# Three norm passages of a two-layer decoder: late squares go to the sums unadded, and some steps of one half get an order against the other half's

## The chip, the cores and the metric

The kernel runs on one core of a Trainium2 chip. The metric is the time of one execution on the device, in microseconds (us). TensorE is called PE below, its weight loads PEld, VectorE DVE, ScalarE ACT, GpSimd POOL, and SyncE, which issues the loads from memory, SP.

## The reference

A trunk of two layers over 512 tokens of width 1024, in float32. Each layer has a token mixer (layer 0: a diagonal state space and a gated linear recurrence side by side; layer 1: gated linear attention, GLA) and a SwiGLU feed-forward part. Each of these sub-layers starts with the same norm, and ends in a gated addition to the trunk `x`:

```python
def rms_norm(x, g):
    xf = x.astype(jnp.float32)
    y = xf * lax.rsqrt(jnp.mean(xf * xf, axis=-1, keepdims=True) + EPS)
    return (y * g.astype(jnp.float32)).astype(x.dtype)

def modulate(h, shift, scale):
    return h * (1 + scale[:, None, :]) + shift[:, None, :]
...
def swiglu(h, w1, w3, w2):
    return (jax.nn.silu(h @ w1) * (h @ w3)) @ w2
```

So between two sub-layers the sum of 1024 squares of each token has to be complete before the first product of the next sub-layer can be formed. `shift`, `scale` and the gate come from a conditioning vector.

## The kernel before

The trunk is held transposed: eight tiles `x0` to `x7` of 128 features by 512 tokens. Products are emulated float32: each weight and each activation is split into a high and a low part (`hi`, `lo`; `whi`, `wlo`; `hhi`, `hlo`), and three matmuls are made of them, hi by hi (line 275), hi by the activation's low part (276) and low weight by high activation (277). In the stretches of this case a matmul has 256 tokens, half of the sequence; `TH` are the two halves, z = 0 and z = 1, called the first and the second half.

Three norm passages are built by `norm_mod` and `norm_stats`, one for each half: f0, from the output projection of layer 0's mixer to its feed-forward part; m1, from that part to GLA; f1, from GLA's output projection to the second feed-forward part. The last two digits of a name give passage and half, so `nst_f01` is f0's second half. The steps of one half:

1. The projection's products end (`or`, or `f` in m1), DVE adds them to the trunk (`residual`, rows `x<-or,mod,x`), and ACT squares each of the eight tiles, `m` = 0 to 7 (line 86, `nsq`; the first two into the two halves of `na`).
2. Squares 2 to 6 are added into the two sums of `na` on POOL or DVE (line 107, `ttv`); square 7 is left as it is.
3. Three statistic parts (the two sums and square 7) go through PE against a matrix of ones and zeros `eb` (line 341, `nst<-eb,na` and `nst<-eb,nsq`). Each part is two matmuls, which run in two passes each, so the trace shows four records for a part.
4. ACT takes the root (`nrs`, line 86), DVE the reciprocal and one Newton step (`nnv`, reciprocal, `nnt`, `nnt`, `nrs`), and DVE writes the result on diagonals (`ndg`, line 111). A matmul against ones spreads them over the partitions (line 347, `nst<-ndg,ones`); it is called the spread below.
5. For each of the eight tiles DVE forms `hf`, ACT `hhi`, DVE `hlo` (lines 116, 86, 116), and the next products take them. In f0 and f1 the first of these are `f1` and `f3` (the two SwiGLU inputs, `whi_f`), in m1 `ga`, `gq` and `gk`.

The order of each engine's instructions isn't written out: a scheduler places them by priorities, by the order in the program and by its own timeline, and each engine then works its list in that order. `tc.issue_after` (used through `after`) and a manual dependency hold one instruction behind another on the list. ACT's function tables are loaded by `tact`, which keeps the table loads (line 101) and the functions that need them in a chain, `table["last"]`; the root of the norm is one such function, the next one is the SiLU of the feed-forward part or of GLA's gate. The squares and the sums of a half come from a pool of four buffers (tags "n" and "X"), the statistics of a half from PSUM.

In `out_rest` (f0 and f1) the whole weight is there when the halves begin; the first half's four pairs of tiles are projected, then `then` builds the first half's norm, then the second half follows.

Of the kernel before, what the change touches and what calls it, by code (L numbers as in the profile page):

```python
# [41 lines left out]
def trunk(  # L42
# [10 lines left out]
    out = out[0]  # L53
# [11 lines left out]
    def tt(name, tag, shape=(P, T), dtype=F32):  # L65
        return tp.tile(list(shape), dtype, tag=tag, name=name, bufs=SLOTS[tag])
# [4 lines left out]
    def const(name, shape, dtype=F32):  # L71
        return cp.tile(list(shape), dtype, name=name, tag=name)

    def mm_ps(name, shape=(P, T)):
        return pm.tile(list(shape), F32, tag="mm", name=name)

    def ps_a(name, shape=(P, T)):
        return pa.tile(list(shape), F32, tag="a", name=name)
# [4 lines left out]
    V, A, G, PE = nc.vector, nc.scalar, nc.gpsimd, nc.tensor  # L83

    def act(o, i, f, **kw):
        return A.activation(out=o, in_=i, func=f, **kw)  # L86

    table = {"set": None, "last": None}
    order = mybir.DependencyInfo(mybir.DependencyClass.NoSync, mybir.DependencyReason.DATA)
# [16 lines left out]
    def ttv(e, o, a, b, op):  # L106
        e.tensor_tensor(out=o, in0=a, in1=b, op=op)  # L107

    def tsv(e, o, a, s1, op0, s2=None, op1=None):
        if s2 is None:  # L110
            e.tensor_scalar(out=o, in0=a, scalar1=s1, scalar2=None, op0=op0)
        else:
            e.tensor_scalar(out=o, in0=a, scalar1=s1, scalar2=s2, op0=op0, op1=op1)

    def stt(o, a, s, b, op0, op1):
        V.scalar_tensor_tensor(out=o, in0=a, scalar=s, in1=b, op0=op0, op1=op1)  # L116


    cs = const("cs", [P, P + 2])
# [1 line left out]
    ident = cs[:, 0:P]  # L121
# [25 lines left out]
    ones = const("ones", [P, P])  # L147
    G.memset(ones, 1.0)
    eb = const("eb", [P, NB, NB])
# [17 lines left out]
    gsc = const("gsc", [P, 4, KT])  # L167
# [65 lines left out]
    def ada_need(*ps):  # L233
        while not done.issuperset(ps):
            next(ada)
# [3 lines left out]
    xT = [xp.tile([P, T], F32, name=f"x{m}", tag=f"x{m}") for m in range(KT)]  # L239
# [18 lines left out]
    def split(e, src, name, th, tl):  # L258
        hi = tt(f"hi_{name}", th, dtype=F32R)
        lo = tt(f"lo_{name}", tl, dtype=F32R)  # L260
        act(hi, src, AF.Copy)
        ttv(e, lo, src, hi.bitcast(F32), ALU.subtract)
        return hi, lo
# [5 lines left out]
    def proj(ps, ws, acts, ts=slice(0, T), ks=None):  # L269

        n = len(ws)
        for i, ((hi, lo), (ah, al)) in enumerate(zip(ws, acts, strict=True)):
            if ks and i not in ks:
                continue
            PE.matmul(ps, lhsT=hi, rhs=ah[:, ts], start=(i == 0), stop=False)  # L275
            PE.matmul(ps, lhsT=hi, rhs=al[:, ts], start=False, stop=False)  # L276
            ins = PE.matmul(ps, lhsT=lo, rhs=ah[:, ts], start=False, stop=(i == n - 1))  # L277
        return ins
# [29 lines left out]
    def inv_rms(name, ss, n, table=True):  # L308

        rs, t, v = (sm(f"{name}{i}", ss.shape) for i in ("rs", "nt", "nv"))  # L310
        if table:
            tact(rs, ss, AF.Sqrt, scale=1.0 / n, bias=eps)
        tsv(V, v, ss, 1.0 / n, ALU.mult, EPS, ALU.add)
        if table:
            V.reciprocal(out=rs, in_=rs)
        else:

            tsv(V, t.bitcast(I32), v.bitcast(I32), 1, ALU.logical_shift_right)
            tsv(V, rs.bitcast(I32), t.bitcast(I32), -1.0, ALU.mult, float(0x5F3759DF), ALU.add)
        for _ in range(1 if table else 3):  # L320
            ttv(V, t, rs, rs, ALU.mult)
            stt(t, t, -0.5, v, ALU.mult, ALU.mult)
            stt(rs, t, 1.5, rs, ALU.add, ALU.mult)
        return rs

    def norm_stats(name, z):

        ts, nb, pst, tag = TH[z], NB // 2, (ps_a, ps_b)[z], "nX"[z]
        sums = tt(f"na_{name}", tag, (P, 2, T // 2))
        for m in range(KT):  # L330
            sq = sums[:, m] if m < 2 else tt(f"nsq_{name}{m}", tag, (P, T // 2))
            act(sq, xT[m][:, ts], AF.Square)
            if 1 < m < KT - 1:
                i = int(m not in (2, 4))
                ttv(V if i and not z else G, sums[:, i], sums[:, i], sq, ALU.add)
        parts = [sums[:, 0], sums[:, 1], sq]
        ps = pst(f"nst_{name}", (P, nb + 1, P))
        rb, st = ps[:, 0:nb, :], ps[:, nb, 0:nb]
        for i, q in enumerate(parts):
            for b in range(nb):  # L340
                PE.matmul(st, lhsT=q[:, b * P : (b + 1) * P], rhs=eb[:, b, 0:nb],
                          start=(i == 0 and b == 0), stop=(i == len(parts) - 1 and b == nb - 1))
        rs = inv_rms("n", st, D)
        dg = tt(f"ndg_{name}", tag, (P, nb, P))
        for b in range(nb):
            tsv(V, dg[:, b, :], ident, rs[:, b : b + 1], ALU.mult)
            PE.matmul(rb[:, b, :], lhsT=ones, rhs=dg[:, b, :], start=True, stop=True)
        return rb.rearrange("p b t -> p (b t)")

    def norm_parts(name):  # L350
        hh = hp.tile([P, KT, T], F32R, tag="h", name=f"hhi_{name}", bufs=2)
        hl = hp.tile([P, KT, T], F32R, tag="h", name=f"hlo_{name}", bufs=2)
        return [(hh[:, m, :], hl[:, m, :]) for m in range(KT)]
# [9 lines left out]

    def norm_mod(q, l, base, name, parts, z):

        ada_need((l, base // 8), (l, base // 8 + 1))
        rb = norm_stats(f"{name}{z}", z)
        ts = TH[z]
        for m in range(KT):
            hh, hl = (i[:, ts] for i in parts[m])  # L370
            shift = mod[:, l, base + m : base + m + 1]
            hf = tt(f"hf_{name}{z}{m}", "nX"[z], (P, T // 2))
            stt(hf, rb, gsc[:, q, m : m + 1], xT[m][:, ts], ALU.mult, ALU.mult)
            act(hh, hf, AF.Identity, bias=shift)
            stt(hl, hf, shift, hh.bitcast(F32), ALU.add, ALU.subtract)

    def ada_first_loads(half):
        tags = iter("s" * 15 + "n")
        ws = []
        for k in range(KT):  # L380
            for i in (1, 0):
                w = tt(f"ar0{i}{half}{k}", next(tags))
                nc.sync.dma_start(out=w, in_=ada_w[0, k * P : (k + 1) * P, i * D + half * T : i * D + half * T + T])
                ws.append(w)
        return ws

    def after(ins):
        return tc.issue_after(ins.ins) if ins is not None else nullcontext()
# [504 lines left out]
    def out_rest(w, ys, l, then):  # L893

        n = len(ys)
        ws = []
        for k in range(n):
            raw = wp.tile([P, D], F32, tag="raw", name=f"raw_or{l}{k}", bufs=3)
            nc.sync.dma_start(out=raw, in_=w[D - (n - k) * P : D - (n - k - 1) * P, :])
            ws.append([split(V, raw[:, i * T : (i + 1) * T], f"or{l}{k}{i}", "s", "s") for i in range(D // T)])  # L900
        for z, ts in enumerate(TH):
            for m in range(0, KT, 2):
                ps = mm_ps(f"or{l}{m}{z}", (P, 2, T // 2))
                for j in (m, m + 1):
                    c = slice(j * P % T, j * P % T + P)
                    proj(ps[:, j - m], [tuple(q[:, c] for q in ws[k][j * P // T]) for k in range(n)], ys, ts)
                for j in (m, m + 1):
                    residual(ps[:, j - m], j, l, 2, ts)
            then(KT - 1, z)

    def then_norm(q, l, base, name, res):

        res += norm_parts(name)

        def then(m, z):
            if m == KT - 1 and z is not None:
                norm_mod(q, l, base, name, res, z)

        return then

# [24 lines left out]
    for m in range(KT):  # L945
        ps = mm_ps(f"xps{m}")
# [10 lines left out]
    for m in range(KT):  # L957
        ps = (mm_ps if m < 4 else ps_b)(f"xnps{m}")
# [9 lines left out]
    second = range(4, KT)  # L968
# [127 lines left out]
    ys = s5_glu(yfs)  # L1096
# [29 lines left out]
    ps = ps_a("ga1")  # L1126
# [20 lines left out]
    for hd in range(4):  # L1147
        ps = mm_ps(f"ga2{hd}")
# [12 lines left out]
        for i, z in enumerate((Q, K)):  # L1161
            ps, w = qk[i] if hd == 0 else gla_qk(hd, i)
# [98 lines left out]
```

## Time and profile before

| | us |
|---|---|
| Three timed runs | 1345.32, 1347.97, 1352.27 |
| Their median | 1347.97 |
| Profiled execution, own time | 1345.65 |
| Its span, first to last instruction | 1343.9 |
| PE busy in the span | 1280.0 |

All times of rows are microseconds from the start of the span of the profiled execution. In a row of the timeline the first number is the start, the second how long the group lasted, `x4` the number of records put together, and the bracket the idle time of that engine ahead of the row with what ended it. Matmuls overlap in their pipeline: a lone matmul of 256 columns shows 0.28 long, while the next one starts 0.12 after it, so what a step takes of PE is read from start to start.

### The profile page before, as it was taken

The numbers are of one execution on the slowest core, as the hardware profiler recorded it, in microseconds if no ns is written. First come the engines' busy times: TensorE is split into PE (matmuls) and PEld (weight loads), VectorE is DVE, ScalarE is ACT, GpSimd is POOL, SyncE is SP. The second block draws the span as 40 slices with busy tenths as digits, with TensorE's granted clock in tenths as the row PEclk, the third lists the DMA queues.
The fourth block names the chain that finished last, engine by engine and source line by source line (L and its number), as shares of the span: only waits on it lengthen the run. The fifth ranks groups of instructions, "written<-read, shape, count | busy, mean of one in ns | idle before, by whom it ended". The sixth has DMA issues, their size and how long they took to land.

```text
span 1343.9 us, 18265 instructions
## 1 busy us (share of the span) xinstructions
PE 1280.0 (95%) x6949; PEld 1097.6 (82%) x6949; DVE 766.8 (57%) x1433; ACT 514.1 (38%) x939; POOL 141.4 (11%) x148
## 2 busy tenths in 40 slices
PE   7797999899999999999999999999899999999997
PEld 3577887778888888888888999997888888888886
DVE  5786995787765566566356446657743333333344
ACT  5477358534522222232244433433432222222322
POOL 0593451110100000000010000000100000000000
PEclk9798998999999999999999999999799999999999
DMA  9742531633097669996250322114033323333232
GB/s 305 173 126 79 157 110 38 152 98 102 20 223 189 186 183 230 205 219 185 74 157 21 102 65 78 56 48 133 17 98 103 97 71 99 113 99 104 65 92 79
DMA packets 222824, 159.69 MB, mean 119 GB/s; under 512 B 16752, under 2 KB 195248, under 8 KB 222736
## 3 DMA queue, kind: packets, MB, share of 16 engines
q1 hardware_dynamic: 221696, 157.48, 43.3%
q8 instruction: 54, 0.88, 0.3%
q10 hardware_dynamic: 1040, 1.05, 0.3%
q14 instruction: 34, 0.28, 0.1%
HBM read 156.40 MB, written 2.10 MB: 118 GB/s over the span
## 4 chain that ended last, share of the span: by engine, by line
PE 81%; DVE 10%; ACT 3%; DMA 3%; issue 2%; SPq 0%; POOL 0%; DVEq 0%; ACTq 0%
PE f L275 18%; PE f L276 18%; PE f L277 18%; DMA ar<-in_ada_w_dram 2%; PE op L276 2%; PE lv_g L465 2%; PE op L277 2%; PE op L275 2%; ACT yf L86 1%; PE gr L300 1%; PE gr L301 1%; PE gv L301 1%; PE gr L299 1%; PE gv L300 1%; PE gv L299 1%
## 5 line engine op out<-in xcount | busy, mean ns | idle before, releaser
L276 PE MATMUL f<-hlo_f,whi_f 128*128 128x512 f32 (+1 forms) x736 | 280.8, 383 | 0.4 <-DVE hlo_f L116 0.4
L275 PE MATMUL f<-hhi_f,whi_f 128*128 128x512 f32 (+1 forms) x736 | 279.9, 383 | 0.9 <-ACT hhi_f L86 0.9
L277 PE MATMUL f<-hhi_f,wlo_f 128*128 128x512 f32 (+1 forms) x736 | 280.1, 382 | 0.0
L86 ACT ACTIVATE whi_f<-raw_f 128x1024 fp32r<-128x1024 f32 x88 | 93.3, 1061 | 309.3 <-PE f L276 167.4
L107 DVE TENSOR_TENSOR wlo_f<-raw_f,whi_f 128x1024 fp32r<-128x1024 f32 x88 | 107.7, 1224 | 113.9 <-ACT whi_f L86 113.2
L276 PEld LDWEIGHTS f<-hlo_f,whi_f 128*128 128x128 f32 x736 | 139.2, 189 | 27.2 <-DVE hlo_f L116 1.4
L275 PEld LDWEIGHTS f<-hhi_f,whi_f 128*128 128x128 f32 x736 | 138.9, 190 | 27.5 <-ACT hhi_f L86 1.4
L277 PEld LDWEIGHTS f<-hhi_f,wlo_f 128*128 128x128 f32 x736 | 139.3, 189 | 26.4
L204 DVE SCALAR_TENSOR_TENSOR acc<-ar,cond,acc 128x512 f32<-128x512 f32 x154 | 122.9, 798 | 39.9 <-DMA ar<-in_ada_w_dram 37.8
L277 PE MATMUL f<-hi_g,wlo_c 128*128 128x512 f32 x312 | 121.8, 390 | 0.0
L276 PE MATMUL f<-lo_g,whi_c 128*128 128x512 f32 x312 | 121.7, 390 | 0.0
L275 PE MATMUL f<-hi_g,whi_c 128*128 128x512 f32 x312 | 121.3, 390 | 0.0
L86 ACT ACTIVATE whi_c<-raw_c 128x768 fp32r<-128x768 f32 (+1 forms) x56 | 44.8, 801 | 161.9 <-PE f L276 107.7
L107 DVE TENSOR_TENSOR g<-g,f 128x512 f32<-128x512 f32 x44 | 30.2, 687 | 106.1 <-PE f L277 106.0
L107 DVE TENSOR_TENSOR wlo_c<-raw_c,whi_c 128x768 fp32r<-128x768 f32 (+1 forms) x56 | 50.3, 898 | 60.6 <-ACT whi_c L86 59.1
L275 PEld LDWEIGHTS f<-hi_g,whi_c 128*128 128x128 f32 x312 | 58.6, 188 | 12.1
L276 PEld LDWEIGHTS f<-lo_g,whi_c 128*128 128x128 f32 x312 | 58.6, 188 | 12.1
L277 PEld LDWEIGHTS f<-hi_g,wlo_c 128*128 128x128 f32 x312 | 58.6, 188 | 12.0
L116 DVE SCALAR_TENSOR_TENSOR x<-f,mod,x 128x512 f32<-128x512 f32 (+1 forms) x36 | 24.8, 689 | 40.5 <-PE f L277 40.4
L107 POOL TENSOR_TENSOR na_m<-na_m,nsq_m 128x256 f32<-128x256 f32 x7 | 5.9, 856 | 361.7 <-ACT nsq_m L86 361.7
L300 PE MATMUL gv<-wlo_gv,hhi_m 128*128 128x256 f32 x128 | 36.7, 287 | 0.0
L301 PE MATMUL gv<-whi_gv,hlo_m 128*128 128x256 f32 x128 | 36.6, 287 | 0.0
(668 smaller groups left out, 2651.8 us busy)
## 6 DMA issues: line engine op xcount, KB each, us to landing
raw_f<-in_ffn_w_dram SPq DMA_DIRECT2D x88, 512.0 KB, 4.0
ar<-in_ada_w_dram SPq DMA_DIRECT2D x256, 128.0 KB, 4.2
ar<-in_ada_w_dram SPq DMA_DIRECT2D x64, 256.0 KB, 5.4
raw_c<-in_ffn_w_dram SPq DMA_DIRECT2D x32, 384.0 KB, 3.5
raw_c<-in_ffn_w_dram SPq DMA_DIRECT2D x24, 320.0 KB, 3.2
raw_gv<-in_od_w_in_dram SPq DMA_DIRECT2D x8, 512.0 KB, 3.7
raw_gr<-in_od_w_in_dram SPq DMA_DIRECT2D x8, 512.0 KB, 4.5
raw_o<-in_ev_w_out_dram SPq DMA_DIRECT2D x8, 384.0 KB
```

Source lines behind the costliest of these rows:

```text
L86: return A.activation(out=o, in_=i, func=f, **kw)
L107: e.tensor_tensor(out=o, in0=a, in1=b, op=op)
L116: V.scalar_tensor_tensor(out=o, in0=a, scalar=s, in1=b, op0=op0, op1=op1)
L204: ins = V.scalar_tensor_tensor(out=acc, in0=w, scalar=c_, in1=acc, op0=ALU.mult, op1=ALU.add)
L275: PE.matmul(ps, lhsT=hi, rhs=ah[:, ts], start=(i == 0), stop=False)
L276: PE.matmul(ps, lhsT=hi, rhs=al[:, ts], start=False, stop=False)
L277: ins = PE.matmul(ps, lhsT=lo, rhs=ah[:, ts], start=False, stop=(i == n - 1))
L299: PE.matmul(o, lhsT=ah[:, s], rhs=hi, start=(k == 0), stop=False)
L300: PE.matmul(o, lhsT=ah[:, s], rhs=lo, start=False, stop=False)
L301: PE.matmul(o, lhsT=al[:, s], rhs=hi, start=False, stop=(k == KT - 1))
L465: PE.matmul(ps[0:nk, w, :].rearrange("p (n b) -> p n b", b=b), lhsT=K[:, w * P : w * P + nk], rhs=qv[:, w * nb : (w + 1) * nb, b:], start= ...
```

## The change

Four edits. (1) In `norm_stats` squares 2 and 3 alone are added, both on POOL; squares 4 to 7 go to PE as statistic parts of their own, so that a half has six parts where it had three. (2) In `out_rest` the second half's products of tiles 4 and 5 are held behind the last statistic matmul of the first half, those of tiles 6 and 7 behind its spread. (3) The second half's residuals of tiles 4 and 5 are held behind the first half's diagonals, those of 6 and 7 behind its second `hf`. (4) The last `hhi` of the second half is put into the chain of the table loads, so that the next table load comes behind it. Over the whole program the lists of PE grow by the 36 matmuls of 18 added parts, DVE and POOL lose nine additions each, and SP's list of loads is the same.

```diff
     def tsv(e, o, a, s1, op0, s2=None, op1=None):
         if s2 is None:
-            e.tensor_scalar(out=o, in0=a, scalar1=s1, scalar2=None, op0=op0)
+            return e.tensor_scalar(out=o, in0=a, scalar1=s1, scalar2=None, op0=op0)
...
     def stt(o, a, s, b, op0, op1):
-        V.scalar_tensor_tensor(out=o, in0=a, scalar=s, in1=b, op0=op0, op1=op1)
+        return V.scalar_tensor_tensor(out=o, in0=a, scalar=s, in1=b, op0=op0, op1=op1)
...
         sums = tt(f"na_{name}", tag, (P, 2, T // 2))
+        late = []
         for m in range(KT):
             sq = sums[:, m] if m < 2 else tt(f"nsq_{name}{m}", tag, (P, T // 2))
             act(sq, xT[m][:, ts], AF.Square)
-            if 1 < m < KT - 1:
-                i = int(m not in (2, 4))
-                ttv(V if i and not z else G, sums[:, i], sums[:, i], sq, ALU.add)
-        parts = [sums[:, 0], sums[:, 1], sq]
+            if 1 < m < 4:
+                ttv(G, sums[:, m - 2], sums[:, m - 2], sq, ALU.add)
+            elif m >= 4:
+                late.append(sq)
+        parts = [sums[:, 0], sums[:, 1]] + late
...
-                PE.matmul(st, lhsT=q[:, b * P : (b + 1) * P], rhs=eb[:, b, 0:nb],
-                          start=(i == 0 and b == 0), stop=(i == len(parts) - 1 and b == nb - 1))
+                stat = PE.matmul(st, lhsT=q[:, b * P : (b + 1) * P], rhs=eb[:, b, 0:nb],
+                                 start=(i == 0 and b == 0), stop=(i == len(parts) - 1 and b == nb - 1))
...
-            tsv(V, dg[:, b, :], ident, rs[:, b : b + 1], ALU.mult)
-            PE.matmul(rb[:, b, :], lhsT=ones, rhs=dg[:, b, :], start=True, stop=True)
-        return rb.rearrange("p b t -> p (b t)")
+            diag = tsv(V, dg[:, b, :], ident, rs[:, b : b + 1], ALU.mult)
+            spread = PE.matmul(rb[:, b, :], lhsT=ones, rhs=dg[:, b, :], start=True, stop=True)
+        return rb.rearrange("p b t -> p (b t)"), (stat, spread), diag
...
-        rb = norm_stats(f"{name}{z}", z)
+        rb, pes, diag = norm_stats(f"{name}{z}", z)
...
-            stt(hf, rb, gsc[:, q, m : m + 1], xT[m][:, ts], ALU.mult, ALU.mult)
-            act(hh, hf, AF.Identity, bias=shift)
+            ins = stt(hf, rb, gsc[:, q, m : m + 1], xT[m][:, ts], ALU.mult, ALU.mult)
+            if m == 1:
+                second = ins
+            ins = act(hh, hf, AF.Identity, bias=shift)
             stt(hl, hf, shift, hh.bitcast(F32), ALU.add, ALU.subtract)
+        if z:
+            tc.add_manual_dep(ins.ins, table["last"].ins.name, order, reason="table sets in order")
+            table["last"] = ins
+        return pes, (diag, second)
...
+        ins = None
         for z, ts in enumerate(TH):
             for m in range(0, KT, 2):
                 ps = mm_ps(f"or{l}{m}{z}", (P, 2, T // 2))
-                for j in (m, m + 1):
-                    c = slice(j * P % T, j * P % T + P)
-                    proj(ps[:, j - m], [tuple(q[:, c] for q in ws[k][j * P // T]) for k in range(n)], ys, ts)
-                for j in (m, m + 1):
-                    residual(ps[:, j - m], j, l, 2, ts)
-            then(KT - 1, z)
+
+                with after(ins[0][m // 2 - 2] if ins and m > 2 else None):
+                    for j in (m, m + 1):
+                        c = slice(j * P % T, j * P % T + P)
+                        proj(ps[:, j - m], [tuple(q[:, c] for q in ws[k][j * P // T]) for k in range(n)], ys, ts)
+                with after(ins[1][m // 2 - 2] if ins and m > 2 else None):
+                    for j in (m, m + 1):
+                        residual(ps[:, j - m], j, l, 2, ts)
+            ins = then(KT - 1, z)
...
             if m == KT - 1 and z is not None:
-                norm_mod(q, l, base, name, res, z)
+                return norm_mod(q, l, base, name, res, z)
```

PE at f0, from the last products of the output projection to the first of the feed-forward part. `or041` is the second half's projection of tiles 4 and 5, `or061` of tiles 6 and 7. Before:

```order
L277 MATMUL or061_3361<-hi_y_h30_2855,lo_or011_3180 128x256
L341 MATMUL nst_f01_3396<-eb_108,na_f01_3376 128x2 x2
L347 MATMUL nst_f00_3263<-ndg_f00_3279,ones_106 128x128 x2
L341 MATMUL nst_f01_3396<-eb_108,na_f01_3376 128x2 x2
L341 MATMUL nst_f01_3396<-eb_108,nsq_f017_3394 128x2 x2
L275 MATMUL f1_00_3457<-hhi_f0_3161,whi_f1_00_3453 128x256
L275 MATMUL f3_00_3464<-hhi_f0_3161,whi_f3_00_3460 128x256
L276 MATMUL f1_00_3457<-hlo_f0_3162,whi_f1_00_3453 128x256
```

Now:

```order
L277 MATMUL or041_3349<-hi_y_h30_2855,lo_or011_3180 128x256
L343 MATMUL nst_f01_3396<-eb_108,na_f01_3379 128x2 x2
L349 MATMUL nst_f00_3260<-ndg_f00_3282,ones_106 128x128 x2
L275 MATMUL or061_3364<-hi_y_h20_2853,hi_or001_3169 128x256
...
L277 MATMUL or061_3364<-hi_y_h30_2855,lo_or011_3180 128x256
L343 MATMUL nst_f01_3396<-eb_108,na_f01_3379 128x2 x2
L343 MATMUL nst_f01_3396<-eb_108,nsq_f014_3388 128x2 x2
L343 MATMUL nst_f01_3396<-eb_108,nsq_f015_3390 128x2 x2
L275 MATMUL f1_00_3463<-hhi_f0_3161,whi_f1_00_3459 128x256
L275 MATMUL f3_00_3470<-hhi_f0_3161,whi_f3_00_3466 128x256
L276 MATMUL f1_00_3463<-hlo_f0_3162,whi_f1_00_3459 128x256
```

The twelve products of `or061` have moved from ahead of the first half's spread to behind it, and three of the second half's six parts stand between them and the feed-forward part's first products; the parts of squares 6 and 7 come later, among the first half's products.

PE at f0, around the spread of the second half. The first products of the second half are the `L275` rows that stand last. Before:

```order
L275 MATMUL f3_00_3464<-hhi_f0_3161,whi_f3_00_3460 128x256
L347 MATMUL nst_f01_3396<-ndg_f01_3412,ones_106 128x128 x2
L276 MATMUL f1_00_3457<-hlo_f0_3162,whi_f1_00_3453 128x256
L277 MATMUL f1_00_3457<-hhi_f0_3161,wlo_f1_00_3455 128x256
L276 MATMUL f3_00_3464<-hlo_f0_3162,whi_f3_00_3460 128x256
L277 MATMUL f3_00_3464<-hhi_f0_3161,wlo_f3_00_3462 128x256
L275 MATMUL f1_00_3457<-hhi_f0_3161,whi_f1_00_3453 128x256
L275 MATMUL f3_00_3464<-hhi_f0_3161,whi_f3_00_3460 128x256
L275 MATMUL f1_01_3575<-hhi_f0_3161,whi_f1_01_3571 128x512
```

Now:

```order
L276 MATMUL f1_00_3463<-hlo_f0_3162,whi_f1_00_3459 128x256
L277 MATMUL f1_00_3463<-hhi_f0_3161,wlo_f1_00_3461 128x256
L276 MATMUL f3_00_3470<-hlo_f0_3162,whi_f3_00_3466 128x256
L277 MATMUL f3_00_3470<-hhi_f0_3161,wlo_f3_00_3468 128x256
L349 MATMUL nst_f01_3396<-ndg_f01_3418,ones_106 128x128 x2
L275 MATMUL f1_00_3463<-hhi_f0_3161,whi_f1_00_3459 128x256
L275 MATMUL f3_00_3470<-hhi_f0_3161,whi_f3_00_3466 128x256
L275 MATMUL f1_01_3581<-hhi_f0_3161,whi_f1_01_3577 128x512
```

The four products of the first half that stood behind the spread now stand ahead of it, so nothing is between the spread and the second half's first product; f1 has the same order. In m1 nineteen products stood there, and six stand there now.

DVE at f0, from the second half's residuals (`x`) through the first half's Newton step to its first `hf`. Before:

```order
L116 SCALAR_TENSOR_TENSOR x5_146<-or041_3346,mod_131,x5_146 128x256
L113 TENSOR_SCALAR nnv_3272<-nst_f00_3263 128x2
L315 RECIPROCAL nrs_3270<-nrs_3270 128x2
L107 TENSOR_TENSOR nnt_3271<-nrs_3270 128x2
L116 SCALAR_TENSOR_TENSOR nnt_3271<-nnt_3271,nnv_3272 128x2
L116 SCALAR_TENSOR_TENSOR nrs_3270<-nnt_3271,nrs_3270 128x2
L116 SCALAR_TENSOR_TENSOR x6_147<-or061_3361,mod_131,x6_147 128x256
L111 TENSOR_SCALAR ndg_f00_3279<-cs_82,nrs_3270 128x128 x2
L116 SCALAR_TENSOR_TENSOR x7_148<-or061_3361,mod_131,x7_148 128x256
L116 SCALAR_TENSOR_TENSOR hf_f000_3284<-nst_f00_3263,gsc_132,x0_141 128x256
```

Now:

```order
L116 SCALAR_TENSOR_TENSOR x3_144<-or021_3334,mod_131,x3_144 128x256
L113 TENSOR_SCALAR nnv_3275<-nst_f00_3260 128x2
L315 RECIPROCAL nrs_3273<-nrs_3273 128x2
L107 TENSOR_TENSOR nnt_3274<-nrs_3273 128x2
L116 SCALAR_TENSOR_TENSOR nnt_3274<-nnt_3274,nnv_3275 128x2
L116 SCALAR_TENSOR_TENSOR nrs_3273<-nnt_3274,nrs_3273 128x2
L111 TENSOR_SCALAR ndg_f00_3282<-cs_82,nrs_3273 128x128 x2
L116 SCALAR_TENSOR_TENSOR x4_145<-or041_3349,mod_131,x4_145 128x256
L116 SCALAR_TENSOR_TENSOR x5_146<-or041_3349,mod_131,x5_146 128x256
L116 SCALAR_TENSOR_TENSOR hf_f000_3287<-nst_f00_3260,gsc_132,x0_141 128x256
```

The residual that stood between the Newton step and the diagonals is gone from there; residuals 4 and 5 now follow the diagonals, and 6 and 7 come among the first `hlo`.

## Rows read from the trace of the kernel before

**Rows 1.** The page: busy time by engine, then the chain that ended last.

```profile
PE 1280.0 (95%) x6949; PEld 1097.6 (82%) x6949; DVE 766.8 (57%) x1433; ACT 514.1 (38%) x939; POOL 141.4 (11%) x148
...
PE 81%; DVE 10%; ACT 3%; DMA 3%; issue 2%; SPq 0%; POOL 0%; DVEq 0%; ACTq 0%
```

**Rows 2.** Timeline of PE in m1: two statistic parts, then the next product.

```profile
706.16 0.95 PE L341 MATMUL nst_m<-eb,na_m 128*128 128x2 f32 x8
706.97 0.36 PE L275 MATMUL f<-hi_g,hi_d 128*128 128x256 f32 x1
```

**Rows 3.** Timeline of PE in f0, first half's spread to second half's first products.

```profile
343.04 0.28 PE L277 MATMUL or<-hi_y_h,lo_or 128*128 128x256 f32 x1
343.16 0.50 PE L341 MATMUL nst_f<-eb,na_f 128*128 128x2 f32 x4
344.39 0.71 PE L347 MATMUL nst_f<-ndg_f,ones 128*128 128x128 f32 x4 [0.73 <-DVE ndg_f L111]
345.58 0.61 PE L341 MATMUL nst_f<-eb,na_f 128*128 128x2 f32 x4 [0.47 <-POOL na_f L107]
346.04 0.59 PE L341 MATMUL nst_f<-eb,nsq_f 128*128 128x2 f32 x4
346.49 0.49 PE L275 MATMUL f<-hhi_f,whi_f 128*128 128x256 f32 x2
347.25 0.39 PE L276 MATMUL f<-hlo_f,whi_f 128*128 128x256 f32 x1 [0.27 <-DVE hlo_f L116]
...
352.79 0.60 PE L347 MATMUL nst_f<-ndg_f,ones 128*128 128x128 f32 x4
...
354.51 0.73 PE L275 MATMUL f<-hhi_f,whi_f 128*128 128x256 f32 x3 [0.64 <-ACT hhi_f L86]
```

**Rows 4.** Timeline of PE in m1: first half's first products, second half's first product.

```profile
715.13 0.95 PE L341 MATMUL nst_m<-eb,na_m 128*128 128x2 f32 x8
716.29 0.31 PE L1130 MATMUL ga<-hhi_m,a1r 128*32 128x256 f32 x1 [0.21 <-ACT hhi_m L86]
...
717.70 0.31 PE L1130 MATMUL ga<-hlo_m,a1r 128*32 128x256 f32 x1 [0.87 <-DVE hlo_m L116]
...
725.80 0.28 PE L1130 MATMUL ga<-hhi_m,a1r 128*32 128x256 f32 x1
```

**Rows 5.** Timeline of PE in f1: first half's spread, second half's first products.

```profile
961.25 0.50 PE L341 MATMUL nst_f<-eb,na_f 128*128 128x2 f32 x4
963.15 1.47 PE L347 MATMUL nst_f<-ndg_f,ones 128*128 128x128 f32 x4 [1.39 <-DVE ndg_f L111]
...
976.22 0.64 PE L275 MATMUL f<-hhi_f,whi_f 128*128 128x256 f32 x3
```

**Rows 6.** Windows: bounds, length, busy by engine, PE clock, DMA share, GB/s.

```profile
734.00:739.00 5.00, 3.85 (x31) 3.81 (x32) 3.70 (x4) 4.94 (x8) 0.00 (x0) 1.00 0.18 48
...
963.30:973.40 10.10, 9.78 (x41) 8.95 (x42) 8.07 (x25) 5.47 (x11) 0.38 (x1) 0.50 0.00 1
973.50:983.50 10.00, 10.00 (x74) 9.46 (x74) 5.98 (x16) 3.35 (x8) 0.00 (x0) 1.00 0.19 54
```

**Rows 7.** Timeline of DVE: a Newton step's row in f0, m1 and f1.

```profile
342.90 0.66 DVE L116 SCALAR_TENSOR_TENSOR nnt<-nnt,nnv 128x2 f32<-128x2 f32 x1
...
710.79 0.16 DVE L107 TENSOR_TENSOR nnt<-nrs 128x2 f32<-128x2 f32 x1
...
960.96 0.69 DVE L107 TENSOR_TENSOR nnt<-nrs 128x2 f32<-128x2 f32 x1
```

**Rows 8.** Timeline of POOL: additions of squares in f0 and f1.

```profile
340.65 2.89 POOL L107 TENSOR_TENSOR na_f<-na_f,nsq_f 128x256 f32<-128x256 f32 x4 [3.62 <-ACT nsq_f L86]
...
960.20 1.43 POOL L107 TENSOR_TENSOR na_f<-na_f,nsq_f 128x256 f32<-128x256 f32 x2 [0.52 <-ACT nsq_f L86]
```

**Rows 9.** Timeline of ACT in f0: table load, and the next work behind the passage.

```profile
347.14 1.28 ACT L101 ACT_TABLE_LOAD   x1
...
363.35 1.06 ACT L86 ACTIVATE whi_f<-raw_f 128x1024 fp32r<-128x1024 f32 x1 [3.77 <-PE f L276]
```

More of the change, by code (lines that the diff above doesn't have):

```diff
@@ L110, in tsv @@
         if s2 is None:
-            e.tensor_scalar(out=o, in0=a, scalar1=s1, scalar2=None, op0=op0)
+            return e.tensor_scalar(out=o, in0=a, scalar1=s1, scalar2=None, op0=op0)
         else:
-            e.tensor_scalar(out=o, in0=a, scalar1=s1, scalar2=s2, op0=op0, op1=op1)
+            return e.tensor_scalar(out=o, in0=a, scalar1=s1, scalar2=s2, op0=op0, op1=op1)
     def stt(o, a, s, b, op0, op1):
-        V.scalar_tensor_tensor(out=o, in0=a, scalar=s, in1=b, op0=op0, op1=op1)
+        return V.scalar_tensor_tensor(out=o, in0=a, scalar=s, in1=b, op0=op0, op1=op1)
     cs = const("cs", [P, P + 2])
```

## The prediction

> **What bounds the kernel now.** First the page: PE is busy 1280.0 us, 95% of the span, and 81% of the chain that ended last is PE [rows 1]. So a microsecond counts only if PE gains or loses it, and what is added to PE counts in full unless it falls into a wait of PE. Second, the timeline of PE through the passages, since the lists differ only there: which rows have a bracket, and how far a row starts behind the one before it. Third, the windows, for PE's clock in the same stretches. Fourth, the timelines of DVE, POOL and ACT for what PE waited for. The sum below is against the profiled execution's own 1345.65 us.
>
> **The added statistic parts.** 18 parts are added, six a passage. In m1 two parts take PE from 706.16 to 706.97, 0.81 us, so 0.40 each [rows 2]; in f0 the last part before the products takes 346.04 to 346.49, 0.45 [rows 3]. Bounds: nothing for a part that falls into a wait, 0.45 for one that doesn't. Nearly all now stand between products, where PE doesn't wait, so I take 0.40: 18 × 0.40 = 7.2 us, 2.4 a passage. The nine additions taken from DVE and nine from POOL give PE nothing directly; they shorten the way from a square to its sum, which is where the next term is.
>
> **f0.** A product takes PE 0.12 (343.04 to 343.16), and I give the spread, two matmuls like a part, the same 0.40. From row to row PE then loses [rows 3]:
> - before the first half's spread 343.16 to 344.39, less a part: 1.23 − 0.40 = 0.83;
> - behind it, for POOL's last sum, 344.39 to 345.58 less the spread: 1.19 − 0.40 = 0.79;
> - for the first `hlo`, 346.49 to 347.25 less two products: 0.76 − 0.24 = 0.52;
> - for the second half's first `hhi`, 352.79 to 354.51 less the spread and the four products that the list of before has there: 1.72 − 0.40 − 0.48 = 0.84.
>
> The second and third go: twelve products and three parts, 12 × 0.12 + 3 × 0.40 = 2.6 us, now stand between the spread and the first `hhi` product, and the whole way from the spread to the first `hlo` product took 347.25 − 344.39 = 2.86 before, of which the parts and two products are already paid. The first stays. As before, some eleven or twelve products and a part lie between the first half's last statistic and its spread. The residual that stood on DVE between the Newton step and the diagonals is gone, but the Newton step still meets POOL: right behind the root ACT squares tiles 2 and 3 of the second half, and their additions run on POOL while DVE works. In f0 `nnt` took 0.66 with POOL adding from 340.65 to 343.54, in f1 0.69 with POOL adding from 960.20, in m1 0.16 with POOL idle [rows 7, 8]. Bounds: 0 if the residual's place is all that counted, 0.83 if POOL is; I take 0.83, since rows in both passages have POOL beside them. The fourth grows: the four products that lay behind the spread are now ahead of it, so the whole way from spread to `hhi`, 1.72 − 0.40 = 1.32, is a wait. Its cover is gone by the change itself. f0: 2.4 − 0.79 − 0.52 − 0.84 + 1.32 = +1.6.
>
> On that collision there is a rule. The Trainium skill, page "SBUF — State Buffer", section "Who interferes with whom", says that a DVE instruction with two inputs in SBUF contends with a GpSimd instruction that reads SBUF, and that the loser fully blocks. The rows above agree: 128x2 instructions of 0.16 become 0.66 and 0.69 beside POOL. By it the two additions left on POOL still strike the Newton step and the sum stands; without it the first wait would go in f0 and f1 and the sum be 1.7 lower.
>
> **m1.** PE loses 715.13 to 716.29 less two parts, 1.16 − 0.80 = 0.36, before the first `hhi`, and 716.29 to 717.70 less three products, 1.41 − 0.36 = 1.05, before the first `hlo`; it loses nothing at the second half's first product, 725.80, which has no bracket [rows 4]. The first half's products start with more work ready, so both go: −1.41. But of the nineteen products between the second half's spread and its first product six are left, 0.72, against the way of 1.32 read in f0: a wait of 0.60, and behind it the wait for `hlo`, for which I take m1's first bare wait, 0.36. m1: 2.4 − 1.41 + 0.96 = +1.95.
>
> **f1.** Here PE waits 961.25 to 963.15 less a part, 1.50, for the diagonals, and then runs at half clock, 0.50 from 963.30 to 973.40, and at 1.00 behind it [rows 5, 6]. From the first half's spread to the second half's first product it takes 963.15 to 976.22, 13.07 us; f0 takes 10.12 with 0.79 + 0.52 + 0.84 of waits in it, 7.97 without [rows 3, 5]. So the slow stretch, with its own waits, costs 5.1. With the order of f0, and the two residuals gone from DVE's list ahead of the diagonals, the wait before the spread comes to f0's 0.83, a gain of 0.67. A wait of 0.83 in f0 brought no fall of the clock, nor did 1.15 us without PE work in the five of 734 to 739 [rows 6], so I take the clock as kept: −5.1. The second half's first product waits 1.32 as in f0. f1: 2.4 − 0.67 − 5.1 + 1.32 = −2.05. Bounds of the clock term: −5.1 (kept) and 0 (lost as before).
>
> **The table load, the orders.** The load takes 1.28 on ACT, ahead of five `hhi` of the first half in f0. Behind the last `hhi` of the passage ACT then idles 3.77 until the next work [rows 9], so the moved load is hidden there; without that cover it would cost up to 1.28 in each of three passages, 3.8 us. The gain for `hhi` is in the `hlo` waits already counted. The waits added in the output projection stand on PE and DVE behind work of the first half that comes at once; queued behind them are the second half's own products, which PE would only reach after the spread anyway. Squares 6 and 7 of the second half wait for a buffer that the part of square 4 frees; that part stands ahead of the first feed-forward products, and `hhi` of tile 4 is queued behind on ACT; its cover is the 24 products of four tiles, 2.9 us. SP's list does not change, and its loads have no part in these stretches (DMA share 0.00 in f1) [rows 6].
>
> **Sum.** +1.6 + 1.95 − 2.05 = +1.5 us: 1347.2 in the profiled execution's terms. That execution and the three runs have 1345.3, 1345.65, 1348.0 and 1352.3; their middle is 1346.8, so I forecast 1348.3. About 0.5% (6.7 us) is what a measurement of this kernel can tell from no change, so this is "same".
>
> **Rivals.**
> 1. *All waits go, and the clock stays.* If the spread waits of f0 and f1 vanish (−0.83 each beyond the above for f0 and f1) and the second half's first products wait nowhere (−1.32, −0.96, −1.32): 1.5 − 5.3 = −3.8, about 1343. For it: POOL has nine additions fewer and the second half's spread has room to be early. Against: nothing in the list stands between the second half's spread and its first product. If the parts too fell into waits at half their price, −3.6 more, 1339.5: faster.
> 2. *Half clock behind the new waits: slower.* In f1 a wait of 1.50 stands ahead of a half-clock stretch worth 5.1. The new waits before the second half's first products (1.32 in f0 and f1) are near it. If a wait of that size is followed by the clock at 0.50, f0 gains one such stretch and f1 only moves its own: +1.5 + 5.1 + 5.1 = +11.7, 1358.5; if only one of them falls, +6.6, 1353.4. For it: the size of the wait. Against: dense products ahead of these waits, and the 1.15 us idle at 734 to 739 at full clock. It decides from a wait of about 1.3 on.
> 3. *The change doesn't reach the waits.* If the first half's chain stays what ends last in f1 and the clock falls as before: +1.5 + 5.1 + 0.67 = +7.3, 1354: like rival 2's milder end, by another road.
>
> **Chances.** The forecast with its neighbours (waits off by one or two us) 0.70; rival 1 0.15, of which 0.05 below −6.7; rival 2 0.10, of which 0.07 above +6.7; rival 3 0.05, about 0.04 above +6.7. So faster 0.06, same 0.83, slower 0.11. The likeliest case's own range is 1344 to 1352; to hold 8 in 10 with the runs' own spread it reaches to rival 1's middle and rival 2's milder end: 1341 to 1354.
>
> **What would show it.** In the profile after: twelve statistic matmuls a half, about 0.4 us of PE for a part; before the first half's spread in f0 and f1 a wait for `ndg` of 0.7 to 1; no bracket from POOL's sums; clock 1.00 from 963 to 973; a bracket of 1.1 to 1.4 at the second half's first product in f0 and f1, about half that in m1; `nnt` of f0 and f1 above 0.3; the table loads with idle ACT behind them. Wrong it would be if PE falls to half clock behind one of the new waits, if the second half's first products start without a wait, or if statistic parts cost far less than 0.4.

## The result and the profile after

The changed kernel is slower, by 0.8%: 1358.71 us, median of six runs (1357.18 to 1361.24), against 1347.91 (1345.32 to 1352.27); the ratio is 1.0084, 95% interval 1.0065 to 1.0103, +10.8 us. The range ended at 1354.0, so the time lies outside it, near the 1358.5 of the second rival.

The page, busy time by engine, then PE's granted clock in 40 slices:

```profile
PE 1295.2 (95%) x7021; PEld 1114.2 (82%) x7021; DVE 762.0 (56%) x1424; ACT 514.2 (38%) x939; POOL 136.2 (10%) x139
...
PEclk9798989989999999999998999999799999999999
```

PE is 15.2 us busier than before [rows 1], in the same 95% of a longer span: it does not wait more, it works longer. The windows say why. Columns as in [rows 6], the busy times in the order PE, PEld, DVE, ACT, POOL; the first of each pair is the stretch ahead of a fall of the clock, the second the stretch at half clock:

```profile
341.70:345.11 3.41, 3.41 (x32) 3.41 (x32) 1.39 (x4) 1.31 (x4) 0.00 (x0) 1.00 0.02 5
345.11:348.53 3.42, 3.42 (x19) 3.42 (x18) 3.28 (x10) 1.09 (x4) 1.43 (x2) 0.50 0.00 0
710.33:713.75 3.42, 3.42 (x33) 3.42 (x32) 0.48 (x1) 0.42 (x1) 0.00 (x0) 1.00 0.48 150
713.75:720.58 6.83, 6.83 (x34) 6.83 (x34) 1.20 (x7) 0.26 (x1) 0.00 (x0) 0.50 0.01 2
966.33:969.75 3.42, 3.42 (x32) 3.42 (x32) 1.09 (x5) 1.21 (x4) 0.06 (x1) 1.00 0.00 0
969.75:986.82 17.07, 17.07 (x81) 17.05 (x81) 10.96 (x32) 5.51 (x14) 1.37 (x2) 0.50 0.00 1
```

Each of the three passages now has a stretch at 0.50 (1.2 GHz in place of 2.4), 27.3 us together where before had 13.7, all of it in f1. And PE is busy for the whole of the stretch shown ahead of each fall, so no wait stands right ahead of these.

What PE did ahead of them, in its timeline; f0 first:

```profile
342.25 0.50 PE L343 MATMUL nst_f<-eb,na_f 128*128 128x2 f32 x4
342.62 1.48 PE L343 MATMUL nst_f<-eb,nsq_f 128*128 128x2 f32 x12
...
358.12 0.60 PE L349 MATMUL nst_f<-ndg_f,ones 128*128 128x128 f32 x4
...
359.84 0.73 PE L275 MATMUL f<-hhi_f,whi_f 128*128 128x256 f32 x3 [1.12 <-ACT hhi_f L86]
```

m1 and then f1:

```profile
711.49 0.95 PE L343 MATMUL nst_m<-eb,na_m 128*128 128x2 f32 x8
712.30 1.48 PE L343 MATMUL nst_m<-eb,nsq_m 128*128 128x2 f32 x12
...
724.82 0.95 PE L343 MATMUL nst_m<-eb,na_m 128*128 128x2 f32 x8
725.63 1.03 PE L343 MATMUL nst_m<-eb,nsq_m 128*128 128x2 f32 x8
...
734.23 0.60 PE L349 MATMUL nst_m<-ndg_m,ones 128*128 128x128 f32 x4
...
735.95 0.30 PE L1143 MATMUL ga<-hhi_m,a1r 128*32 128x256 f32 x1 [0.40 <-ACT hhi_m L86]
...
966.51 0.50 PE L343 MATMUL nst_f<-eb,na_f 128*128 128x2 f32 x4
966.88 1.48 PE L343 MATMUL nst_f<-eb,nsq_f 128*128 128x2 f32 x12
...
968.42 0.50 PE L343 MATMUL nst_f<-eb,nsq_f 128*128 128x2 f32 x4
...
988.37 0.60 PE L349 MATMUL nst_f<-ndg_f,ones 128*128 128x128 f32 x4
990.18 0.73 PE L275 MATMUL f<-hhi_f,whi_f 128*128 128x256 f32 x3 [1.20 <-ACT hhi_f L86]
```

Four or five statistic parts stand in a row ahead of every fall: the second sum and squares 4 to 6 in f0 (342.25 to 343.96), both sums and three squares in m1, the second sum and all four squares, with one product between, in f1. Not every such row is followed by a fall: the four parts of m1's second half, 724.82 to 726.53, were not. The wait that the second rival blamed comes later, at 358.72 and 988.98, and no fall follows it. In f0 and f1 the waits for POOL's last sum and for the first `hlo` [rows 3] are gone, as forecast.

To set passages apart, the table gives the time between the same PE instructions of each trace: from the first product of the output projection to the 121st product of line 275 on `hhi` in the feed-forward part (f0, f1), and from the first product of the last feed-forward projection to the eleventh product of GLA's values (m1); in brackets the microseconds at 0.50 in it.

| kernel | to f0 | f0 | m1 | f1 | time |
|---|---|---|---|---|---|
| before | 327.90 | 93.49 (0) | 37.71 (0) | 95.75 (13.7) | 1347.91 |
| changed | 331.19 | 95.53 (3.4) | 42.82 (6.8) | 99.95 (17.1) | 1358.71 |
| orders and table load alone (e3) | 328.54 | 93.21 (0) | 42.23 (6.8) | 91.31 (0) | 1346.37 |
| late squares alone (e4) | 329.97 | 97.30 (6.8) | 41.30 (3.4) | 96.07 (10.2) | 1354.93 |
| changed, parts of 128 columns (e5) | 327.68 | 94.98 (0) | 39.81 (0) | 93.11 (0) | 1348.14 |
| before, parts of 128 columns (e6) | 328.86 | 93.21 (0) | 37.78 (0) | 92.39 (0) | 1343.74 |

Up to f0 the lists of all these kernels are alike apart from a constant, yet 327.7 to 331.2 us pass, so the 3.3 us there between before and changed are not the change's. The times were taken in several sessions; before's own median beside e1 to e4 is 1347.01, beside e5 to e8 1347.49, beside e9 and e10 1347.83. The three passages together lost 2.04 + 5.11 + 4.20 = 11.35 us in the profiles, close to the 10.8 of the medians.

Of before's 13.7 us in f1, 3.4 lie ahead of the passage's first statistic part: they begin with its first products, behind two waits.

```profile
945.23 0.44 PE L540 MATMUL yT_g<-cs,y_g 128*128 128x128 f32 x2 [1.31 <-DVE y_g L116]
946.14 1.22 PE L275 MATMUL or<-hi_y_g,hi_or 128*128 128x256 f32 x4 [0.47 <-ACT hi_y_g L86]
```

```profile
946.20:949.50 3.30, 3.30 (x15) 3.30 (x16) 1.45 (x4) 0.38 (x1) 0.00 (x0) 0.50 0.01 2
```

The first 40 products there take 7.07 us in before and 5.77 in the changed kernel. Three of the twelve profiles have this fall (before, e7, e8), the other nine the same waits without it.

### The profile page after: what moved, and what is told of

Its sections match the earlier page's. It is cut to its first block, busy times and chain, and to the rows that moved or that the text cites. A ratio compares the mean times of both kernels' runs of the same rounds, so it can differ in the third digit from the quotient of the medians.

```text
span 1357.9 us, 18374 instructions
## 1 busy us (share of the span) xinstructions
PE 1295.2 (95%) x7021; PEld 1114.2 (82%) x7021; DVE 762.0 (56%) x1424; ACT 514.2 (38%) x939; POOL 136.2 (10%) x139
## 4 chain that ended last, share of the span: by engine, by line
PE 82%; DVE 7%; ACT 4%; DMA 4%; issue 2%; POOL 1%; SPq 0%; DVEq 0%; ACTq 0%; POOLq 0%
PE f L276 18%; PE f L275 18%; PE f L277 18%; DMA ar<-in_ada_w_dram 3%; PE op L275 2%; PE op L276 2%; PE op L277 2%; PE lv_g L474 2%; ACT yf L86 1%; PE gr L300 1%; PE gr L301 1%; PE gr L299 1%; PE gv L301 1%; PE gv L300 1%; PE gv L299 1%
## 5 line engine op out<-in xcount | busy, mean ns | idle before, releaser
L275 PE MATMUL f<-hhi_f,whi_f 128*128 128x512 f32 (+1 forms) x736 | 280.1, 383 | 2.3 <-ACT hhi_f L86 2.3
L275 PEld LDWEIGHTS f<-hhi_f,whi_f 128*128 128x128 f32 x736 | 139.3, 190 | 28.6 <-ACT hhi_f L86 2.7
L275 PE MATMUL f<-hi_g,whi_c 128*128 128x512 f32 x312 | 121.2, 390 | 0.0
L275 PEld LDWEIGHTS f<-hi_g,whi_c 128*128 128x128 f32 x312 | 58.6, 188 | 12.0
L107 POOL TENSOR_TENSOR na_m<-na_m,nsq_m 128x256 f32<-128x256 f32 x4 | 3.1, 786 | 344.2 <-ACT nsq_m L86 344.2
```

## Experiments

Theory 1: a row of statistic parts, 128x2 matmuls with PE busy throughout, brings the half clock. Theory 2, the rival: waits of PE bring it, as the prediction had it.

**e1 and e2: the disputed work by itself.** Ten matmuls, the work of five parts, at four places of the kernel before where PE never waits:

```diff
                     if t:
-                        proj(*ups[-1], h)
+                        ins = proj(*ups[-1], h)
+                if l == 0 and t in (4, 6, 8, 10):
+                    dps = ps_b(f"dum{t}")
+                    with after(ins):
+                        for j in range(10):
+                            PE.matmul(dps[:, 0:2], lhsT=ones, rhs=ones[:, 0:2], start=(j == 0), stop=(j == 9))
```

e2 has 128 for 2.

> The kernel before, with ten extra matmuls of 128x2 (the shape and number of five statistic parts) back to back at four places in the middle of the first feed-forward part, where PE never waits and the clock stays at 1.00; their result is used by nothing. Theory 1 (a row of statistic parts brings PE's half clock, though PE doesn't wait): each place costs five parts, 5 x 0.40 = 2.0 us, and is followed by at least one stretch at 0.50 like the 3.4 us one in f0 of the changed kernel, 1.7 us lost: 4 x 3.7 = +14.8 us, about 1362.7. Theory 2 (only waits of PE bring it): 4 x 2.0 = +8.0 us, about 1356, and no stretch at 0.50 in the feed-forward part.

> As the run with narrow extra matmuls, at the same four places, but each of the ten moves 128 columns and not 2. The spread, two such matmuls, takes PE 0.36 to 0.40 like a part of two columns, so the extra work is again 4 x 2.0 = +8.0 us. Theory 1 (narrow parts count): no stretch at 0.50 there, +8 us, about 1356, well below the narrow run. If a row of float32 matmuls brings the half clock whatever its width: as the narrow run, +14.8. Theory 2 (waits): +8, and the narrow run the same.

Narrow: 1357.35 us, ratio 1.0082 (1.0062 to 1.0102). Wide: 1354.16, ratio 1.0061 (1.0042 to 1.0081). The second place in the narrow kernel, timeline and the window behind it, then the same place in the wide one:

```profile
431.66 2.29 PE L852 MATMUL dum<-ones 128*128 128x2 f32 x20
433.81 0.48 PE L275 MATMUL f<-hhi_f,whi_f 128*128 128x512 f32 x1
```

Windows of the narrow kernel:

```profile
434.86:438.27 3.41, 3.41 (x10) 2.67 (x9) 1.06 (x2) 0.00 (x0) 0.00 (x0) 0.50 0.78 234
```

```profile
431.07 2.39 PE L852 MATMUL dum<-ones 128*128 128x128 f32 x20
433.22 0.48 PE L275 MATMUL f<-hhi_f,whi_f 128*128 128x512 f32 x1
```

Windows of the wide kernel:

```profile
434.00:440.00 6.00, 6.00 (x28) 4.95 (x27) 1.43 (x4) 1.19 (x2) 0.00 (x0) 1.00 0.62 177
```

To the next product a place takes 2.15 us in both, 431.66 to 433.81 and 431.07 to 433.22: narrow matmuls take PE no less than wide ones, 0.43 a part. Of the narrow places one in four was followed by half clock, not each as theory 1 had it; of the wide ones none. The runs lie apart (1356.34 to 1357.90 narrow, 1353.33 to 1355.85 wide), but the intervals of the two ratios overlap, so e8 doubles the row. (The 1.71 us a place that the next expectations use were a slip of mine: a growth divided by four places in a stretch that holds three. It is 2.15, and twice that for twenty.)

> As the run with ten narrow extra matmuls at four places, of which one place of four was followed by a stretch at 0.50, with twenty at each. Theory 1: every place is followed by a stretch at 0.50: 8 x 1.71 = 13.7 us for the work, and 4 x 1.7 to 4 x 3.4 for the clock: +20 to +27 us, 1367 to 1374. Theory 2: +13.7, 1361, and the clock at 1.00.

1377.27 us, ratio 1.0220 (1.0184 to 1.0257), +29.8, above the expected range: 8 × 2.15 = 17.2 for the work, and 20.5 us at half clock, 10.2 lost, make 27.4; 3.4 us at half clock in f0 and 3.4 in m1, where the profile of before had none, add up to 3.4 more. The windows at the four places; at the second and the fourth the clock falls while the row still runs:

```profile
412.43:415.84 3.41, 3.41 (x10) 2.63 (x9) 0.00 (x0) 0.00 (x0) 0.00 (x0) 0.50 0.30 85
439.74:446.56 6.82, 6.82 (x24) 5.85 (x24) 1.08 (x2) 0.00 (x0) 0.00 (x0) 0.50 0.55 154
470.46:473.87 3.41, 3.41 (x10) 2.76 (x10) 0.00 (x0) 0.00 (x0) 0.00 (x0) 0.50 0.87 252
497.77:504.59 6.82, 6.82 (x21) 5.56 (x21) 0.00 (x0) 0.00 (x0) 0.00 (x0) 0.50 0.41 111
```

Four of four, in the middle of a part where before ran at 1.00 throughout, without a wait of PE. With twenty matmuls every place had a fall, with ten one of four, in one profile each.

**e3 and e4: the change taken apart.** e3 has the changed kernel with `norm_stats` adding as before, e4 the kernel before with the late squares alone:

```diff
-            if 1 < m < 4:
-                ttv(G, sums[:, m - 2], sums[:, m - 2], sq, ALU.add)
-            elif m >= 4:
-                late.append(sq)
-        parts = [sums[:, 0], sums[:, 1]] + late
+            if 1 < m < KT - 1:
+                i = int(m not in (2, 4))
+                ttv(V if i and not z else G, sums[:, i], sums[:, i], sq, ALU.add)
+        parts = [sums[:, 0], sums[:, 1], sq]
```

> The changed kernel with the additions of before: three statistic parts a half again, but the orders of the output projection and the table load kept. Theory 1: no new stretch at half clock in f0 and m1; f0 -0.8 us, m1 near 0, f1 between -4.5 (clock kept) and +0.7: 1343 to 1348. Theory 2 (the new waits before the second half's first products bring the half clock): the stretches at 0.50 come in f0 and f1 behind that wait of 1.1 to 1.4 us, and the time is about 1353.

> The kernel before with the late squares alone: six statistic parts a half, no orders, table load as before. Theory 1: five parts stand in a row in f0, m1 and f1, so PE falls to half clock behind them as in the changed kernel, +7.2 for the parts and 3 to 7 for the clock, less some 2 us of waits for POOL: 1356 to 1360. Theory 2: parts alone bring no fall in f0 and m1: +7.2 - 2 = +5, about 1353.

e3: 1346.37 us, ratio 0.9997 (0.9985 to 1.0009), the same as before. e4: 1354.93, ratio 1.0064 (1.0043 to 1.0085). So the late squares carry the loss, with or without the orders. e3 has the waits ahead of the second half's first products, 1.12 in f0 and 1.20 in f1, and no fall in f0 or f1, against theory 2; but it has one in m1, against what theory 1 had:

```profile
715.48 0.95 PE L342 MATMUL nst_m<-eb,na_m 128*128 128x2 f32 x8
716.64 0.31 PE L1142 MATMUL ga<-hhi_m,a1r 128*32 128x256 f32 x1 [0.21 <-ACT hhi_m L86]
...
718.06 0.42 PE L1142 MATMUL ga<-hlo_m,a1r 128*32 128x256 f32 x1 [0.87 <-DVE hlo_m L116]
...
728.65 0.60 PE L348 MATMUL nst_m<-ndg_m,ones 128*128 128x128 f32 x4
730.37 0.31 PE L1142 MATMUL ga<-hhi_m,a1r 128*32 128x256 f32 x1 [1.12 <-ACT hhi_m L86]
```

And the window:

```profile
717.93:724.76 6.83, 6.70 (x33) 6.48 (x34) 5.53 (x19) 2.05 (x6) 0.00 (x0) 0.50 0.00 1
```

There two parts and two waits, 0.21 and 0.87, stand together, as in the profile of before [rows 4], where no fall followed; and f0 of e1 and e2, with before's list there, had 6.8 us at half clock, m1 of e1 3.4, where before had none. Parts and waits stand together there (with the same waits and wide parts, e7 below, m1 has no fall), and the same work is followed by a fall in one execution and not in another. e4 came 1 us below its range. Its fall in f0 came behind six parts, with the spread among them, and in a wait of 2.17, so it does not tell the two apart; but its falls in m1 (715.85) and at 968.44 in f1 came behind rows of five and four parts with PE busy for all of the 3.41 us ahead.

**e5, e6 and e10: the columns alone.** The parts keep their number and nearly their places; each matmul moves 128 columns, one of ones and 127 of zeros:

```diff
+    ew = const("ew", [P, P + 1])
+    G.memset(ew, 0.0)
+    G.memset(ew[:, 1:2], 1.0)
...
-                stat = PE.matmul(st, lhsT=q[:, b * P : (b + 1) * P], rhs=eb[:, b, 0:nb],
+                stat = PE.matmul(ps[:, nb, :], lhsT=q[:, b * P : (b + 1) * P], rhs=ew[:, 1 - b : 1 - b + P],
```

> The changed kernel with the same 36 statistic matmuls a passage in nearly the same places of PE's list, each moving 128 columns (one of ones, 127 of zeros) and not 2. A row of ten such extra matmuls cost PE 1.71 us a place, the narrow ones the same beside the clock. Theory 1 (the rows of narrow parts bring the half clock): the stretches at 0.50 in f0, m1 and f1 that follow five parts in a row (3.4, 6.8 and 17.1 us in the changed kernel) go or shrink to those of before, 13.7 us: -6 us, about 1352.5. Theory 2 (the waits moved to the second half's first products bring them): they stay, about 1358.5.

> The kernel before with its own three parts a half moving 128 columns. Theory 1: half clock around f0, m1 and f1 gets rarer, 0 to -5 us: 1342 to 1347. Theory 2 (waits alone): f1's stretch stays, the time is that of before, 1347.

> The kernel before with its three parts a half moving 128 columns, once more beside the other: 1343.7 as in its first run, 0.3% below the kernel before. Theory 1: no stretch at 0.50 in f0, m1 and f1 in the profile, or fewer than the 13.7 us of before. Theory 2 (waits alone bring the fall): f1's stretch is there again behind a wait of 1.3 us.

(A passage has 24 statistic matmuls; 36 is the number of parts in all.) e5: 1348.14 us, ratio 1.0001 (0.9989 to 1.0013). The changed kernel comes back 10.6 us, more than the 6 expected, and stands level with before. Two rows of its PE timeline:

```profile
339.31 1.50 PE L346 MATMUL nst_f<-ew,nsq_f 128*128 128x128 f32 x12
...
964.55 0.71 PE L352 MATMUL nst_f<-ndg_f,ones 128*128 128x128 f32 x4 [0.31 <-DVE ndg_f L111]
```

Its windows:

```profile
338.50:342.00 3.50, 3.50 (x33) 3.50 (x32) 1.64 (x4) 1.47 (x5) 0.00 (x0) 1.00 0.02 5
342.00:345.50 3.50, 3.15 (x25) 2.76 (x25) 3.36 (x12) 1.30 (x5) 1.42 (x2) 1.00 0.00 0
707.00:720.00 13.00, 13.00 (x114) 12.98 (x114) 5.70 (x18) 3.22 (x8) 0.00 (x0) 1.00 0.13 42
959.00:976.00 17.00, 15.71 (x131) 15.12 (x130) 12.59 (x38) 7.05 (x19) 1.42 (x2) 1.00 0.00 1
```

The same rows of parts, three squares in 1.50 us where narrow ones took 1.48, and the clock stays at 1.00 in all three passages. This is the decisive run: nothing but the columns differs to speak of. It does not hang on one profile: PE's granted clock over the whole execution, noted for every run, is 0.966 to 0.969 in the six runs of the changed kernel and 0.977 to 0.980 in the ten of e5; before's 25 beside e5 have 0.970 to 0.977. And it is not the zeros: e2's columns are all ones, and its clock is 0.974 to 0.976, against 0.971 to 0.972 with two columns (e1).

e6: 1343.74, ratio 0.9970 (0.9955 to 0.9985); again as e10: 1344.43, ratio 0.9975 (0.9962 to 0.9989). Neither profile has a fall in a passage, and f1 goes from 95.75 to 92.39, though the wait ahead of the first half's spread is still there:

```profile
962.65 0.49 PE L350 MATMUL nst_f<-ndg_f,ones 128*128 128x128 f32 x2 [1.28 <-DVE ndg_f L111]
```

Its window over the same stretch:

```profile
959.00:976.00 17.00, 14.04 (x101) 12.34 (x100) 15.23 (x46) 9.71 (x22) 2.42 (x4) 1.00 0.01 1
```

The half clock that before had at this place [rows 5, 6] thus hung on its narrow parts too: the four kernels with this list and narrow parts (before, e1, e2, e8) all have 6.8 to 10.2 us of it from this spread on, e6 and e10 none.

**e7 and e9: orders with wide parts.** e7 is e3 with parts of 128 columns; e9 moves the table load in f0 and f1 alone:

```diff
-        if z:
+        if z and name[0] == "f":
             tc.add_manual_dep(ins.ins, table["last"].ins.name, order, reason="table sets in order")
```

> The kernel with the orders and the table load of the change and the additions of before (which had one 6.8 us stretch at 0.50 in m1), its parts moving 128 columns. Theory 1: that stretch goes in part of the runs, 0 to -3.4 us: 1343 to 1346. Theory 2: 1346.4, as with two columns.

> The kernel before with parts of 128 columns, the orders of the output projection (f0, f1), and the table load moved in f0 and f1 alone, not in m1. In the runs so far, outside stretches at half clock, the orders took f1 from about 92.4 to 91.0 us, left f0 as it was, and with the table load moved in m1 that passage took 39.4 in place of 37.8. If the moved load is what costs m1, this kernel is 1.6 us below the one with the load moved everywhere and 1.4 below the one without any of it: about 1342.3. If the orders cost m1: as e7, 1345.

e7: 1345.30, ratio 0.9990 (0.9976 to 1.0005). e9: 1344.96, ratio 0.9976 (0.9962 to 0.9990). In m1 e7 took 39.37 us and e9 37.79, no fall there in either: the moved load costs m1 1.6. In f1 e7 took 92.69, with the fall of 3.4 us at the passage's first products that before has too. e9 took 92.89, of which some 1.7 are a fall, without which it would be about 91.2. That fall came with wide parts, a little behind a wait:

```profile
973.95 0.74 PE L278 MATMUL f<-hhi_f,whi_f 128*128 128x256 f32 x3 [1.20 <-ACT hhi_f L86]
974.98 0.39 PE L279 MATMUL f<-hlo_f,whi_f 128*128 128x256 f32 x1 [0.29 <-DVE hlo_f L116]
```

And the window:

```profile
975.99:979.40 3.41, 3.41 (x12) 2.92 (x11) 3.27 (x9) 2.96 (x5) 0.00 (x0) 0.50 0.05 16
```

So falls come behind waits as well, with no narrow part near; theory 2 is wrong only as the whole cause. e7's time fits either theory. e9 did not reach the 1342.3 expected of it, though its m1 did gain the 1.6, and it is not below e6 in time: the 1.2 us that the orders give in f1 is less than the runs can tell. e6, with one edit, is as fast as any kernel here and beats both the kernel before and the changed one.

## Why the prediction was wrong

The step that failed is the clock term of f1: "A wait of 0.83 in f0 brought no fall of the clock, nor did 1.15 us without PE work in the five of 734 to 739 [rows 6], so I take the clock as kept: −5.1." It looked for the cause of a fall in waits alone, and had none in f0 and m1. The runs showed in its place that rows of 128x2 parts bring the fall though PE is busy (e8, 4 of 4 places), and that the same parts with 128 columns don't (e5). The change doubles such parts and lets them gather: squares 4 to 6 wait for the second sum and then run at once.

- **The parts' own time**, 0.40 each: 18 × 0.40 = 7.2, is near what e1 and e2 measure, 0.43 each, 7.7.
- **Everything but the clock** was close, in f1 by luck. e5 has the change at full clock; against before, f0 is +1.49 (forecast +1.6), m1 +2.10 (+1.95), f1 −2.64 (−2.05, with the clock kept), +0.95 in all against +1.5. But 1.3 of the −2.64 is the fall at before's first products of f1, which the forecast left out; without it f1 gained 1.3. The 5.1 for keeping the clock was too much: e6, with before's list at full clock, takes 86.6 us behind those 40 products where before takes 88.7, a gain of 2.1, since PE waits there instead (busy 14.04 of 17.00). The changed kernel is 0.55, 3.01 and 6.84 above e5 in the three passages, 10.4 together: the whole of the miss.
- **First half's spread.** I kept 0.83 of wait in f0 and f1, from start to start. At full clock e5 has 343.08 to 344.11 in f0, less 0.45 for a part: 0.58, and 0.57 in f1. Its bracket, 0.73 and 1.39 before, is 0.55 and 0.57 with the orders alone (e3) and 0.31 in both with the late squares too (e5). So the orders, the residual's place among them, gave the most in f1, the late squares the rest. The collision with POOL that the forecast put there was seen. DVE, then POOL, in f0 of the changed kernel:

```profile
345.64 0.72 DVE L107 TENSOR_TENSOR nnt<-nrs 128x2 f32<-128x2 f32 x1
346.40 0.66 DVE L116 SCALAR_TENSOR_TENSOR nnt<-nnt,nnv 128x2 f32<-128x2 f32 x1
```

```profile
345.61 1.43 POOL L107 TENSOR_TENSOR na_f<-na_f,nsq_f 128x256 f32<-128x256 f32 x2 [5.79 <-ACT nsq_f L86]
```

Before, in f0, the second took 0.66 as well [rows 7], but the first only 0.36:

```profile
342.50 0.36 DVE L107 TENSOR_TENSOR nnt<-nrs 128x2 f32<-128x2 f32 x1
```

The rule of the Trainium skill, page "SBUF — State Buffer", section "Who interferes with whom", agrees with these rows: each of the two takes 0.66 or 0.72 beside POOL, against 0.16 without.

- **Second half's first products.** Forecast 1.32, 0.60 and 1.32 of loss; 358.12 to 359.84 less 0.40 is 1.32, 734.23 to 735.95 less 0.40 and six products is 0.60, 988.37 to 990.18 less 0.40 is 1.41. Right.
- **The table load.** It has its cover in f0:

```profile
364.92 1.28 ACT L101 ACT_TABLE_LOAD   x1
368.68 1.06 ACT L86 ACTIVATE whi_f<-raw_f 128x1024 fp32r<-128x1024 f32 x1 [2.47 <-PE f L276]
```

In m1 I put the load at nothing and read only the list (six products left of nineteen, 0.96 with the wait for `hlo`). e7 against e9, with three parts a half, shows 1.6 us for moving it there. The load itself isn't late, ACT idles behind it; with it moved, the scheduler placed the second half's spread behind the last of the first half's products, so that a wait of 1.12 follows it. With six parts the move hardly shows: e4, which leaves it out, takes 41.30 in m1, some 39.6 without its 3.4 us at half clock (an estimate, half of them lost), against 39.81 in e5.

- **The rivals.** Rival 2 had the time, 1358.5, by luck, with the wrong cause: in the changed kernel no fall follows the waits of 1.12 and 1.20 that it named. Rival 3 was right for f1, where the clock falls still, but not for its reason: the wait ahead of the spread did shrink.

Left open: why f1's stretch of 17.1 us in the changed kernel lasts so much longer than the others. Eleven of f1's twelve parts lie in or just ahead of it, those of the second half from 970.73 to 982; but f0's second half has its parts too, 347.18 to 354, and the clock was back at 348.53 and stayed. A kernel with the second half's parts alone widened was not run.

## What to carry to other kernels

Before adding narrow matmuls to a dense stretch, count them as a risk to PE's clock as if they were waits, not only at their own time: a part of 2 columns cost 0.43 us on PE, and rows of them some 10 us of this kernel through the clock (e5). Where a matmul takes no longer for more columns, let it move more, even of zeros; here that cost nothing (five parts in a row 2.15 us narrow, 711.49 to 713.64, and 2.16 wide in e5) and gave 0.3% without any other edit (e6, e10). And price a clock term by what PE did in the whole stretch ahead of a fall, over more than one profile: the same list fell in one execution and not in the next.

## What the runs showed of the hardware that was not expected

- A float32 matmul of 128x128 weights takes PE the same with 2 columns as with 128: ten in 2.15 us either way (e1, e2). Their twenty weight loads take 2.43 us on PEld in both.
- PE at 100% busy can be granted half clock: 3.41 of 3.41 us busy at 1.00 in f0, with matmuls of 2 and of 256 columns, then 3.42 at 0.50.
- How much half clock one execution gets varies: ahead of f0, with the same list on PE, the twelve profiles have 47.8 to 58.0 us of it and take 327.7 to 331.2 us. The two don't go together: e5 and e7 both have 47.8, and take 327.7 and 331.2.
